# The last gate of a hybrid decoder layer as seven block products

## The chip, the core and the metric

The kernel runs on one core of a Trainium2 chip. TensorE (PE) multiplies out of the on-chip memory SBUF into the banks of PSUM; VectorE (DVE) and ScalarE (ACT) read PSUM and work elementwise in SBUF; GpSimd (POOL) does small work and issues DMAs; SyncE (SP) issues DMAs. Each engine takes its instructions in the order in which they were recorded and waits for the others by semaphores. The metric is the device time of one execution in microseconds (us). Three runs of the kernel before took 959.69, 959.97 and 960.47 us; their median is 959.97.

## What is computed

One layer on 512 tokens of 1024 features in float32: a gated linear attention beside a dilated window attention, an MLP with squared ReLU, and a gated embedding. The part that the change touches is the end:

```python
x = x + jnp.square(jax.nn.relu(h2 @ w_mlp1[i])) @ w_mlp2[i]
h3 = rmsnorm(x, ln3[i])
x = x + jax.nn.sigmoid(h3 @ w_pg[i]) * (p[i] @ w_pp[i])
return rmsnorm(x, ln_f)
```

`w_pg` is 1024 x 1024 and `w_pp` 256 x 1024. The norm of `h3` is applied late: `x * ln3` goes through the product, and the factor of each token goes into the scale of the sigmoid.

## The kernel before

**Three products for one.** Each float32 operand is split into a high part (`hi`, rounded by an ACT copy) and a low part (`lo`, a DVE subtraction), and a product is the sum of hi·hi, lo·hi and hi·lo. A weight unit is 128 x 1024: SP loads it into one of 6 raw buffers, ACT writes `hi` (L280), DVE writes `lo` (L275). `fetch` records these for one unit after the other as the products come to them, two to three units ahead.

**Seven products for eight.** Where both operands split into 2 x 2 blocks, the kernel takes Strassen's form with seven block products (`strassen`; `wide` where the weight is the moving operand and a tile has 128 tokens by 512 features). The price is sums of blocks: of weights (a DMA that adds on landing, issued by POOL at L242 and L257, or a DVE addition at L254 and L260), and of the input (`T1` to `T4`, each with splits of its own). The seven products of `wide` share the six PSUM banks of the groups a, c (pool `mm`, 4 banks, tiles `mmt`) and b (pool `sm`, tiles `smt`). A result that is finished by a later product is first copied to SBUF (`begin`) and completed by an addition from PSUM (`add`, L421).

**The order of the work.** `run` records matmuls in pieces and calls `step()` after each. A step takes one item of `later` (small work on a result) and, when enough columns have gone by, one stage of the generators in `side` (up to a `yield`). So a piece of work on ACT or DVE has a fixed place in its engine's queue, and what stands behind it waits.

**The end of the kernel before.** The second MLP product's sums go into `xx` (`finals`, L1458 and L1459). `normed` then splits each of the 8 tiles of `x * ln3` in `later`: ACT writes `hi` with the scale (L430) and a square (L461), DVE `lo` (L438) and the sum of squares (L1271). Beside the embedding product `pp` (8 tiles of 128 tokens by 512 features, 6 matmuls each, evacuated by ACT at L1531), `to_tokens` transposes `x` to tokens on PE (L1547) and ACT copies it (L1550). A `pp` tile takes one of the 4 `mm` banks; the first four take the banks that `finals` reads, the last four those of the first four. The gate `pg` is two groups of 512 features (`tmaj`), each of 4 token tiles of 24 matmuls; every tile is finished by itself: sigmoid (L1563), product with `pp` and sum (L1569, L1570), square with a row sum (L1574), and for the second group the final factor (L1590, POOL's power at L1591) and two scaled outputs (L1593 on ACT, L1599 on DVE). The last tile is cut into 384 and 128 features.

Of the kernel before, what the change touches and what calls it, by code (L numbers as in the profile page):

```python
# [19 lines left out]
P = 128  # L20
# [26 lines left out]
def weight_units():  # L47
# [7 lines left out]
    def tm(name, src, col):  # L55
        for i in range(4):
            u.append((f"{name}.{i}", "tm", src, i * 2 * P, col))

# [39 lines left out]
    for j in range(2):  # L98
        tm(f"pg{j}", "w_pg", j * 512)
# [74 lines left out]

LAST = 384
# [5 lines left out]
def block_kernel(ctx, tc, xT, ws, pT, wts, wha, wa2, vec, lnf, rel, onehot, ident_d, mask_d, out):  # L181
# [201 lines left out]
    def wide(name, xo, finish):  # L383
# [13 lines left out]
        for i, (op, xname, b) in enumerate(WIDE):  # L397
# [3 lines left out]
            for pr in range(4):  # L401
                wh, wl = weight(f"{name}.{op}.{pr // 2}")
                xh, xl = xo(xname, pr)
                r = slice((pr % 2) * 512, (pr % 2 + 1) * 512)
                mms = []
                for n in range(2):
                    c = slice(n * P, (n + 1) * P)
                    for k, (l, w) in enumerate(((xh, wh), (xl, wh), (xh, wl))):
                        mms.append((bank[b][n], l[:, c], w[:, r], fresh and not pr and not k, pr == 3 and k == 2))
                run(mms, 3, shared=True)  # L410
# [849 lines left out]

    def normed(j, col, res, acc):
# [291 lines left out]

    side.append(to_tokens())
    for g in range(2):
        tmaj(f"pp{g}", pt, evac_pp)
    ss2 = const.tile([P, 12], F32, name="ss2")
    sp2 = const.tile([P, 4], F32, name="sp2")
    fr = const.tile([P, 4], F32, name="fr")

    def gate(ps, n, tt):
        sg = u32()
        S.activation(sg[:, 0:n], ps[:, 0:n], AF.Sigmoid, scale=rt3[0][:, tt:tt + 1])  # L1563
        return sg

    def gated(sg, i, c):

        n = c.stop - c.start
        V.tensor_tensor(sg[:, 0:n], sg[:, 0:n], pps[i][:, c], op=OP.mult)  # L1569
        V.tensor_tensor(x2t[i][:, c], x2t[i][:, c], sg[:, 0:n], op=OP.add)  # L1570

    def squares(sg, i, c, col):
        n = c.stop - c.start
        S.activation(sg[:, 0:n], x2t[i][:, c], AF.Square, scale=1.0 / 32.0, accum_out=ss2[:, col:col + 1])  # L1574

    def gated_all(ps, i, tt, col):
        sg = gate(ps, 512, tt)
        gated(sg, i, slice(0, 512))
        squares(sg, i, slice(0, 512), col)

    def evac_pg0(tt, ps):
        if len(x2t) < 8:
            drain()
        gated_all(ps, tt, tt, tt)
        V.tensor_scalar(sp2[:, tt:tt + 1], ss2[:, tt:tt + 1], EPS, None, op0=OP.add)
        V.tensor_tensor(x2t[tt], x2t[tt], lnb[0], op=OP.mult)

    def scale_out(tt, col):

        V.tensor_scalar(sp2[:, tt:tt + 1], ss2[:, col:col + 1], sp2[:, tt:tt + 1], None, op0=OP.add)  # L1590
        GP.tensor_tensor(fr[:, tt:tt + 1], sp2[:, tt:tt + 1], mh[:, 0:1], op=OP.pow)  # L1591
        o = u32()
        S.activation(o, x2t[tt], AF.Copy, scale=fr[:, tt:tt + 1])  # L1593
        (S if tt == 3 else SY).dma_start(out[tt * P:(tt + 1) * P, 0:512], o)

    def put(tt, c):
        n = c.stop - c.start
        o = u32()
# [115 lines left out]
```

## Time and profile before

| | |
|---|---|
| median of three runs | 959.97 us |
| the profiled execution: its own time | 960.32 us |
| its span, first to last instruction | 958.5 us |
| PE busy (share) | 950.3 us (99%) |
| DVE busy | 739.4 us (77%) |
| ACT busy | 542.0 us (57%) |
| POOL busy | 95.3 us (10%) |
| DMA, mean | 148 GB/s |
| granted TensorE clock, mean | 0.998 |

The span is what the trace covers; the execution's own time is 1.82 us longer. A busy time is that of records whose ends are partly modelled, so a busy PE says that a matmul was under way, not how many; the distance between starts gives the rate. Waits are listed by who waited and who released.

### The profile page before, as it was taken

What the parts mean: (1) busy time and instruction counts of PE and PEld (TensorE: products, weight loads), DVE (VectorE), ACT (ScalarE), POOL (GpSimd) and SP (SyncE); (2) the same over time, 40 slices, a digit from 0 to 9 for tenths busy, and PEclk for the clock granted to TensorE, in tenths of its full rate; (3) what the DMA queues carried; (4) which work ended last, traced back from release to release, by engine and by line L of the source; (5) the groups of instructions that cost most, each with busy time, mean ns of one, the idle gap of its engine ahead of it and who ended that gap; (6) DMA issues with size and microseconds to landing.
All of it is one profiled execution on the core that took longest, in us unless ns stands there. A gap on an engine that the chain in (4) does not pass through costs nothing.

```text
span 958.5 us, 15733 instructions
## 1 busy us (share of the span) xinstructions
PE 950.3 (99%) x6230; PEld 869.3 (91%) x6230; DVE 739.4 (77%) x1060; ACT 542.0 (57%) x884; POOL 95.3 (10%) x135
## 2 busy tenths in 40 slices
PE   9999999999999999999999999999999999999997
PEld 8789998899988888999988899999998998988886
DVE  7698879866788689969755798777677899787754
ACT  7357547545674679675723456556566673354733
POOL 0140010130000012031010000101000100000000
PEclk9999999999999999999999999999999999999999
DMA  9484472973727647465645436565653473453102
GB/s 320 125 233 114 127 177 67 308 242 92 174 70 248 157 133 183 112 141 190 165 107 194 129 70 195 133 163 157 171 152 107 122 186 98 137 192 104 44 1 89
DMA packets 43723, 142.00 MB, mean 148 GB/s; under 512 B 6468, under 2 KB 7056, under 8 KB 43649
## 3 DMA queue, kind: packets, MB, share of 16 engines
q1 hardware_dynamic: 28512, 96.42, 30.1%
q0 software_dynamic: 11456, 40.07, 21.2%
q10 hardware_dynamic: 3680, 4.51, 1.3%
q8 instruction: 49, 0.80, 0.3%
q14 instruction: 26, 0.20, 0.1%
HBM read 134.64 MB, written 8.17 MB: 149 GB/s over the span
## 4 chain that ended last, share of the span: by engine, by line
PE 96%; DVE 1%; issue 1%; ACT 1%; DMA 1%; POOL 0%; POOLq 0%; DVEq 0%; ACTq 0%
PE mmt L294 80%; PE smt L294 7%; PE mmt L551 2%; PE smt L985 1%; PE smt L925 1%; PE smt L848 1%; DMA u<-y_dram 1%; PE smt L523 0%; PE smt L818 0%; PE smt L942 0%; PE smt L941 0%; PE smt L931 0%; PE smt L817 0%; PE smt L1547 0%; PE smt L1041 0%
## 5 line engine op out<-in xcount | busy, mean ns | idle before, releaser
L294 PE MATMUL mmt<-ur,hi 128*128 128x256 f32 (+1 forms) x2896 | 594.8, 303 | 0.0
L294 PEld LDWEIGHTS mmt<-ur,hi 128*128 128x128 f32 x2896 | 465.9, 188 | 21.8
L294 PE MATMUL mmt<-ur,lo 128*128 128x256 f32 (+1 forms) x1448 | 438.9, 303 | 0.0
L275 DVE TENSOR_TENSOR lo<-w,hi 128x1024 fp32r<-128x1024 f32 x250 | 303.5, 1219 | 52.3 <-PE mmt L294 30.2
L280 ACT ACTIVATE hi<-w 128x1024 fp32r<-128x1024 f32 x250 | 261.1, 1054 | 105.3 <-PE mmt L294 30.0
L294 PEld LDWEIGHTS mmt<-ur,lo 128*128 128x128 f32 x1448 | 272.7, 188 | 10.9
L294 PE MATMUL mmt<-hi,ur 128*128 128x512 f32 (+3 forms) x576 | 162.5, 367 | 0.0
L428 ACT ACTIVATE ur<-u 128x512 fp32r<-128x512 f32 x122 | 72.3, 624 | 96.8 <-DVE u L1248 30.9
L294 PEld LDWEIGHTS mmt<-hi,ur 128*128 128x128 f32 x576 | 102.5, 188 | 15.9
L294 PE MATMUL mmt<-lo,ur 128*128 128x512 f32 (+3 forms) x288 | 105.0, 365 | 0.0
L421 DVE TENSOR_TENSOR u<-u,mmt 128x512 f32<-128x512 f32 (+1 forms) x112 | 70.2, 655 | 37.1 <-PE mmt L294 36.9
L436 DVE TENSOR_TENSOR ur<-u,ur 128x512 fp32r<-128x512 f32 x121 | 79.5, 685 | 16.6 <-ACT ur L428 16.2
L368 ACT ACTIVATE u<-mmt 128x512 f32<-128x512 f32 x80 | 47.4, 593 | 47.6 <-PE mmt L294 47.3
L242 POOL DMA_DIRECT2D w<-in_wts_dram x34 | 31.3, 959 | 335.1 <-DMA w<-in_wts_dram 139.0
L294 PEld LDWEIGHTS mmt<-lo,ur 128*128 128x128 f32 x288 | 54.2, 188 | 8.6
L257 POOL DMA_DIRECT2D w<-in_wts_dram x22 | 19.6, 889 | 319.2 <-DVE w L254 231.1
L294 PE MATMUL smt<-ur,hi 128*128 128x512 f32 x160 | 50.4, 393 | 0.1
L294 PEld LDWEIGHTS smt<-ur,hi 128*128 128x128 f32 x160 | 29.7, 188 | 8.1 <-PE smt L648 0.8
L294 PE MATMUL smt<-ur,lo 128*128 128x512 f32 x80 | 31.2, 390 | 0.0
L254 DVE TENSOR_TENSOR w<-w 128x1024 f32<-128x1024 f32 x22 | 27.0, 1225 | 0.8
L260 DVE TENSOR_TENSOR w<-w 128x1024 f32<-128x1024 f32 x22 | 27.0, 1225 | 0.8
L461 ACT ACTIVATE u<-u 128x512 f32<-128x512 f32 x24 | 14.9, 621 | 16.7 <-DVE u L1329 16.7
(214 smaller groups left out, 793.2 us busy)
## 6 DMA issues: line engine op xcount, KB each, us to landing
w<-in_wts_dram SPq DMA_DIRECT2D x172, 512.0 KB, 4.4
w<-in_wts_dram POOLq DMA_DIRECT2D x56, 512.0 KB, 5.7
u<-in_xT_dram SPq DMA_DIRECT2D x8, 256.0 KB, 5.3
u<-in_ws_dram SPq DMA_DIRECT2D x8, 256.0 KB, 5.4
v_dram<-u ACTq DMA_DIRECT2D x8, 256.0 KB, 8.9
u<-v_dram POOLq DMA_DIRECT2D x8, 256.0 KB, 7.0
y_dram<-u ACTq DMA_DIRECT2D x8, 256.0 KB, 3.9
u<-y_dram POOLq DMA_DIRECT2D x8, 256.0 KB, 6.0
```

The costliest lines, as they stand in the source:

```text
L242: GP.dma_start(w, wts[UNIT[b]], accum_op=OP.add)
L254: V.tensor_tensor(w, w, raw[f"{q}.A11"], op=OP.add)
L257: GP.dma_start(w, wts[UNIT[f"{q}.A21"]], accum_op=OP.add)
L260: V.tensor_tensor(w, w, raw[f"{q}.A12"], op=OP.add)
L275: V.tensor_tensor(lo, w, hi.bitcast(F32), op=OP.subtract)
L280: S.activation(hi, w, AF.Copy)
L294: TE.matmul(o, lhsT=l, rhs=r, start=a, stop=b, skip_group_check=shared)
L368: S.activation(sums[c], bank[b], AF.Copy, scale=-scale if c[0] else scale)
L421: V.tensor_tensor(out, s, ps, op=OP.subtract if m else OP.add)
L428: S.activation(hi, x, AF.Copy)
L436: V.tensor_tensor(lo, x, hi.bitcast(F32), op=OP.subtract)
L551: TE.matmul(q0ps[i], lhsT=(hi, hi, lo)[j][:, c], rhs=(xh, xl, xh)[j], start=not k and not j, stop=k == KC - 1 and j == 2)
```

## The change

The gate becomes one `wide` group over all 1024 features: seven products of 24 matmuls of 512 columns. Its weights are 8 units of another layout, of which two are also loaded a second time and four are added to on landing, and its input sums are made by a new generator `x2sums` in `side`. `normed` keeps the scaled tile `xc` in float32 for that, and splits only the first half of the tokens where the other half is not needed. Each result's finish becomes a chain in `later`. The last product goes token tile by token tile. `gla_out`, far earlier, gets one more `yield` between its multiplications and its transposes.

```diff
-    for j in range(2):
-        tm(f"pg{j}", "w_pg", j * 512)
+    quadw("pg", "w_pg", (0, 512))
...
-    def wide(name, xo, finish):
+    def wide(name, xo, finish, by_tile=False):
...
+            last = by_tile and i == len(WIDE) - 1
+            for ns in ((0,), (1,)) if last else ((0, 1),):
+                for pr in range(4):
...
+                if last:
+                    later.append(end(*WEND[i][0], ns[0], b))
...
             if p % 2:
                 yield
+        yield
         for f in range(2):
...
+        h = slice(0, T if j % 2 else HT)
+
         def first():
-            hi, sq = split_hi(x, c), square(x)
+            xc[j] = u32()
+            S.activation(xc[j], x, AF.Copy, scale=c)
+            sq, hi, lo = square(x), u32r(), u32r()
+            S.activation(hi[:, h], xc[j][:, h], AF.Copy)
 
             def second():
-                res[j] = split_lo(x, hi, c)
+                V.tensor_tensor(lo[:, h], xc[j][:, h], hi[:, h].bitcast(F32), op=OP.subtract)
+                res[j] = hi, lo
...
+    def x2sums():
...
+        def splits(name, ts):
+            yield
+            his = [split_hi(t) for t in ts]
+            yield
+            for g in range(2):
+                t2x[name, g] = split_lo(ts[g], his[g])
+            yield
+
+        sums(lambda g, o, b11, b12, b21, b22: V.tensor_tensor(t1[g][:, o], b11, b12, op=OP.subtract))
+        yield from splits("T1", t1)
...
+    side.append(x2sums())
     side.append(to_tokens())
...
-    def evac_pg1(tt, ps):
-        gated_all(ps, 4 + tt, tt, 4 + tt)
-        scale_out(tt, 4 + tt)
-        put(tt, slice(0, 512))
-
-    tmaj("pg0", x2s, evac_pg0)
-    tmaj("pg1", x2s, evac_pg1, tts=range(3))
...
+    def gate(m, t, n, s, ps):
+
+        tt = 2 * t + n
+        i = 4 * m + tt
+        if s is None:
+            sg, z, r = u32(), ps, rtn
+            V.tensor_scalar(rtn[:, tt:tt + 1], rt3[0][:, tt:tt + 1], -1.0 if m else 1.0, None, op0=OP.mult)
+        else:
+            add(m, s, s, ps)
+            sg, z, r = s, s, rt3[0]
+
+        def gated():
+            V.tensor_tensor(sg, sg, pps[i], op=OP.mult)
+            V.tensor_tensor(x2t[i], x2t[i], sg, op=OP.add)
+            later.append(squares)
...
+        S.activation(sg, z, AF.Sigmoid, scale=r[:, tt:tt + 1])
+        later.append(gated)
+
+    wide("pg", x2_op, gate, by_tile=True)
+    flush()
```

Where this puts instructions is seen in three places. Line numbers are those of each program. The first is ACT's queue between the last tile of `normed` and the split of the gate's first weights; before (L430 `hi`, L461 squares, L1550 token copies, L1531 evacuations of `pp`, L280 weights):

```order
L430 ACTIVATE ur<-u,cv 128x512
L461 ACTIVATE u<-u 128x512
L1550 ACTIVATE u<-smt 128x512
L1531 ACTIVATE u<-mmt 128x512
L1550 ACTIVATE u<-smt 128x512
L1531 ACTIVATE u<-mmt 128x512
L1550 ACTIVATE u<-smt 128x512
L1531 ACTIVATE u<-mmt 128x512
L1550 ACTIVATE u<-smt 128x512
L280 ACTIVATE hi<-w 128x1024 x2
```

and now (L1272 the scaled copy `xc`, L1274 its `hi`, L1540 evacuations, L1559 token copies, L428 the `hi` of T1, L273 weights):

```order
L1272 ACTIVATE u<-u,cv 128x512
L461 ACTIVATE u<-u 128x512
L1274 ACTIVATE ur<-u 128x512
L1540 ACTIVATE u<-mmt 128x512
L1559 ACTIVATE u<-smt 128x512
L1540 ACTIVATE u<-mmt 128x512
L428 ACTIVATE ur<-u 128x512 x2
L1540 ACTIVATE u<-mmt 128x512
L1559 ACTIVATE u<-smt 128x512
L273 ACTIVATE hi<-w 128x1024 x2
L1540 ACTIVATE u<-mmt 128x512 x2
```

A tile has three ACT passes where it had two, and the third and fourth evacuations stand behind the `hi` of T1 and two weight splits. The second place is DVE's queue from the last addition of squares to the gate's first weights; before (L438 `lo`, L1271 squares, L275 weights, L455 the norm's factor):

```order
L438 SCALAR_TENSOR_TENSOR ur<-u,cv,ur 128x512
L1271 TENSOR_TENSOR u<-u 128x512
L275 TENSOR_TENSOR lo<-w,hi 128x1024 x2
L455 TENSOR_SCALAR rv<-smt 128x4
L275 TENSOR_TENSOR lo<-w,hi 128x1024 x2
```

and now (L1584 and L579 the sums T1 and T2, L436 the `lo` of a sum, L244 a weight sum):

```order
L1277 TENSOR_TENSOR ur<-u,ur 128x512
L1280 TENSOR_TENSOR u<-u 128x512
L1584 TENSOR_TENSOR u<-u 128x256 x4
L268 TENSOR_TENSOR lo<-w,hi 128x1024 x2
L436 TENSOR_TENSOR ur<-u,ur 128x512 x2
L579 SCALAR_TENSOR_TENSOR u<-u 128x256 x4
L268 TENSOR_TENSOR lo<-w,hi 128x1024
L244 TENSOR_TENSOR w<-w 128x1024
L436 TENSOR_TENSOR ur<-u,ur 128x512 x2
L268 TENSOR_TENSOR lo<-w,hi 128x1024
```

The sums and their splits stand between the weights' `lo`. The third place is DVE's end; before (L1569, L1570 the gate, L1590 and L1622 the final factor, L1599 an output):

```order
L1599 SCALAR_TENSOR_TENSOR u<-u,fr 128x512
L1569 TENSOR_TENSOR u<-u 128x384
L1570 TENSOR_TENSOR u<-u 128x384
L1569 TENSOR_TENSOR u<-u 128x128
L1570 TENSOR_TENSOR u<-u 128x128
L1622 TENSOR_SCALAR sp_9784<-ss_9783,sp_9784 128x1
L1590 TENSOR_SCALAR sp_9784<-ss_9783,sp_9784 128x1
L1599 SCALAR_TENSOR_TENSOR u<-u,fr 128x256 x2
```

and now, from the sixth product's results on (L1627 the output weights of the first 512 features, L1614 the negated token factor that the last sigmoids read, L1620 and L1621 the gate, L1633 the final factor, L1645 an output):

```order
L1627 TENSOR_TENSOR u<-u 128x512 x2
L1614 TENSOR_SCALAR rtn<-rtok 128x1
L1633 TENSOR_SCALAR sp_9800<-ss_9799,sp_9800 128x1 x2
L1620 TENSOR_TENSOR u<-u 128x512
L1621 TENSOR_TENSOR u<-u 128x512
L1645 SCALAR_TENSOR_TENSOR u<-u,fr 128x512
L1614 TENSOR_SCALAR rtn<-rtok 128x1
L1645 SCALAR_TENSOR_TENSOR u<-u,fr 128x512
L1620 TENSOR_TENSOR u<-u 128x512
L1621 TENSOR_TENSOR u<-u 128x512
L1633 TENSOR_SCALAR sp_9800<-ss_9799,sp_9800 128x1
L1645 SCALAR_TENSOR_TENSOR u<-u,fr 128x512
```

The factor of the last token tile's sigmoid stands behind the output of another tile, and its own chain is followed by one more sum, a power and two halves of an output.

## Rows read from the trace of the kernel before

**Rows 1.** The page: busy time, share and instructions of each engine.

```profile
PE 950.3 (99%) x6230; PEld 869.3 (91%) x6230; DVE 739.4 (77%) x1060; ACT 542.0 (57%) x884; POOL 95.3 (10%) x135
```

**Rows 2.** PE's waits: us in total, times, the longest.

```profile
PE smt L523 <- POOL ones L518: 1.0, 1, 1.0
PE smt L1140 <- DVE u L1133: 0.2, 1, 0.2
```

**Rows 3.** Stretches: length; busy of PE, PEld, DVE, ACT, POOL; PE clock; DMA.

```profile
432.00:470.00 38.00, 37.84 (x318) 37.26 (x317) 35.75 (x49) 24.63 (x41) 2.43 (x4) 1.00 0.62 188
...
891.00:905.70 14.70, 14.70 (x82) 12.52 (x81) 12.33 (x18) 13.50 (x24) 1.95 (x1) 1.00 0.19 68
905.70:944.40 38.70, 38.70 (x177) 32.07 (x176) 18.95 (x29) 15.94 (x28) 1.10 (x2) 1.00 0.04 16
```

**Rows 4.** The chain that ended last, from 890: start, us, what.

```profile
901.18 0.79 PE smt L468 x8
...
907.57 0.87 PE smt L1547 x8
908.44 36.33 PE mmt L294 x160
```

**Rows 5.** ACT in order of time: start, us, line, operation, count.

```profile
881.14 0.71 ACT L430 ACTIVATE ur<-u,cv 128x512 fp32r<-128x512 f32 x1
881.75 0.62 ACT L461 ACTIVATE u<-u 128x512 f32<-128x512 f32 x1
882.27 0.71 ACT L430 ACTIVATE ur<-u,cv 128x512 fp32r<-128x512 f32 x1
...
891.01 0.73 ACT L430 ACTIVATE ur<-u,cv 128x512 fp32r<-128x512 f32 x1 [7.51 <-DVE u L1459]
...
899.42 2.05 ACT L280 ACTIVATE hi<-w 128x1024 fp32r<-128x1024 f32 x2
```

**Rows 6.** DVE in order of time.

```profile
884.42 2.49 DVE L1432 TENSOR_TENSOR u<-u,rstd 128x512 f32<-128x512 f32 x4
886.83 2.77 DVE L1441 TENSOR_TENSOR u<-u 128x256 f32<-128x256 f32 x8
889.51 0.68 DVE L1458 TENSOR_TENSOR u<-mmt,rstd 128x512 f32<-128x512 f32 x1
...
894.82 0.75 DVE L438 SCALAR_TENSOR_TENSOR ur<-u,cv,ur 128x512 fp32r<-128x512 f32 x1
...
899.88 2.36 DVE L275 TENSOR_TENSOR lo<-w,hi 128x1024 fp32r<-128x1024 f32 x2
```

**Rows 7.** PE in order of time: `pp`'s first tile; the cut tile's two ends.

```profile
891.03 0.39 PE L294 MATMUL mmt<-hi,ur 128*128 128x512 f32 x1
...
944.37 0.56 PE L294 MATMUL mmt<-hi,ur 128*128 128x512 f32 x2
...
951.30 0.28 PE L294 MATMUL mmt<-hi,ur 128*128 128x128 f32 x1
```

**Rows 8.** A group by shape over the whole program: busy, mean ns; idle before.

```profile
L1072 ACT ACTIVATE ur<-u 128x256 fp32r<-128x256 f32 x12 | 4.2, 414 | 0.4 <-DVE u L1070 0.4
```

**Rows 9.** The end of a tile and of the program in order of time.

```profile
944.79 0.69 ACT L1563 ACTIVATE u<-mmt,rtok 128x512 f32<-128x512 f32 x1 [0.90 <-PE mmt L294]
945.52 0.69 DVE L1569 TENSOR_TENSOR u<-u 128x512 f32<-128x512 f32 x1 [1.59 <-ACT u L1563]
946.25 0.69 DVE L1570 TENSOR_TENSOR u<-u 128x512 f32<-128x512 f32 x1
946.97 0.63 ACT L1574 ACTIVATE u<-u 128x512 f32<-128x512 f32 x1 [1.48 <-DVE u L1570]
...
947.73 0.21 DVE L1590 TENSOR_SCALAR sp<-ss,sp 128x1 f32<-128x1 f32 x1 [0.79 <-ACT u L1574]
948.02 0.54 POOL L1591 TENSOR_TENSOR fr<-sp,mh 128x1 f32<-128x1 f32 x1 [4.88 <-DVE sp L1590]
...
953.97 0.88 DVE L1599 SCALAR_TENSOR_TENSOR u<-u,fr 128x256 f32<-128x256 f32 x2 [0.66 <-POOL fr L1591]
```

More of the change, by code (lines that the diff above doesn't have):

```diff
@@ L53, in fm @@
             u.append((f"{name}.{j}", "fm", src, row, col + j * P))
-    def tm(name, src, col):
-        for i in range(4):
-            u.append((f"{name}.{i}", "tm", src, i * 2 * P, col))
     def quad(name, src, col, kind="quad", chunk=0):
@@ L173 @@
 NRAW = 6
-LAST = 384
 NWARM = 9
@@ L400, in wide @@
                 bank[b] = [smt() if b == "b" else mmt() for _ in range(2)]
[L401 to L410, printed above, removed]
+            last = by_tile and i == len(WIDE) - 1
+            for ns in ((0,), (1,)) if last else ((0, 1),):
+                for pr in range(4):
+                    wh, wl = weight(f"{name}.{op}.{pr // 2}")
+                    xh, xl = xo(xname, pr)
+                    r = slice((pr % 2) * 512, (pr % 2 + 1) * 512)
+                    mms = []
+                    for n in ns:
+                        c = slice(n * P, (n + 1) * P)
+                        for k, (l, w) in enumerate(((xh, wh), (xl, wh), (xh, wl))):
+                            mms.append((bank[b][n], l[:, c], w[:, r], fresh and not pr and not k, pr == 3 and k == 2))
+                    run(mms, 3, shared=True)
+                if last:
+                    later.append(end(*WEND[i][0], ns[0], b))
+            if last:
+                break
             if i in WBEGIN:
@@ L1556, in block_kernel @@
         tmaj(f"pp{g}", pt, evac_pp)
-    ss2 = const.tile([P, 12], F32, name="ss2")
+    ss2 = const.tile([P, 8], F32, name="ss2")
     sp2 = const.tile([P, 4], F32, name="sp2")
     fr = const.tile([P, 4], F32, name="fr")
[L1561 to L1598, printed above, removed]
-        V.scalar_tensor_tensor(out=o[:, 0:n], in0=x2t[4 + tt][:, c], scalar=fr[:, tt:tt + 1], in1=lnb[1][:, c],
-                               op0=OP.mult, op1=OP.mult)
-        SY.dma_start(out[tt * P:(tt + 1) * P, 512 + c.start:512 + c.stop], o[:, 0:n])
@@ L1620, in block_kernel, with squares, total, put @@
-    squares(sgs[0], 7, parts[0], 8)
-    gated(sgs[1], 7, parts[1])
-    V.tensor_scalar(sp2[:, 3:4], ss2[:, 8:9], sp2[:, 3:4], None, op0=OP.add)
-    squares(sgs[1], 7, parts[1], 9)
-    scale_out(3, 9)
-    put(3, slice(256, 512))
-    put(3, slice(0, 256))
+    rtn = const.tile([P, 4], F32, name="rtn")
+    halves_done = [0] * 4
+    def gate(m, t, n, s, ps):
[11 more added lines that the diff above has]
+            later.append(squares)
+        def squares():
+            S.activation(sg, x2t[i], AF.Square, scale=1.0 / 32.0, accum_out=ss2[:, i:i + 1])
+            if not m:
+                V.tensor_tensor(x2t[i], x2t[i], lnb[0], op=OP.mult)
+            later.append(total)
+        def total():
+            first = not halves_done[tt]
+            halves_done[tt] += 1
+            V.tensor_scalar(sp2[:, tt:tt + 1], ss2[:, i:i + 1], EPS if first else sp2[:, tt:tt + 1], None, op0=OP.add)
+            if not first:
+                GP.tensor_tensor(fr[:, tt:tt + 1], sp2[:, tt:tt + 1], mh[:, 0:1], op=OP.pow)
+                later.append(put)
+        def put():
+            tok, c = slice(tt * P, (tt + 1) * P), fr[:, tt:tt + 1]
+            o = u32()
+            S.activation(o, x2t[tt], AF.Copy, scale=c)
+            (S if tt == 1 else SY).dma_start(out[tok, 0:512], o)
+            for h in ((slice(256, 512), slice(0, 256)) if tt == 1 else (slice(0, 512),)):
+                q = u32()
+                V.scalar_tensor_tensor(out=q[:, h], in0=x2t[4 + tt][:, h], scalar=c, in1=lnb[1][:, h], op0=OP.mult,
+                                       op1=OP.mult)
+                SY.dma_start(out[tok, 512 + h.start:512 + h.stop], q[:, h])
+        S.activation(sg, z, AF.Sigmoid, scale=r[:, tt:tt + 1])
+        later.append(gated)
```

28 lines of the change are left out of this document (19 added, 9 removed).

## The prediction

> **What bounds the kernel now.** I read the page first, then PE's waits, then stretches of the end, and then ACT, DVE and PE in order of time. The page gives PE 950.3 of 958.5 us, all others at most 77% [rows 1]. PE's waits show two entries for the whole program, 1.0 us at the start and 0.2 us at the transpositions of L1140 [rows 2]. So PE is never short of operands, and what is left is its 1 us at the start and the 7 us after its last matmul. The chain says the same: from 908.44 on, 160 matmuls follow each other in 36.33 us, 0.227 us each [rows 4]. A change that takes matmuls away therefore gains, as long as the other engines still finish in PE's shadow. How much shadow there is in the last 70 us I take from the stretches: ACT is busy for 13.50 of the 14.70 us in which `pp` runs (891.0 to 905.7), DVE for 12.33; in the gate itself DVE for 18.95 and ACT for 15.94 of 38.70 [rows 3]. The room is in the gate, not in `pp`.
>
> **What goes on PE.** The gate has 8 tiles of 24 matmuls before, 7 products of 24 now. The missing tile is in effect the one cut in two: its first matmul of 384 columns starts 0.23 us after 944.37 and its last ends at 951.58, so 7.0 us go [rows 7]. The transpositions stay (0.87 us a group with the change of work around it, 0.79 us for the norm's sums [rows 4]); two of the four groups and the sums now fall among the gate's products.
>
> **What comes, by instruction.** ACT: a third pass for each of the 8 tiles of `normed`, 8 `hi` of sums, 6 more weight `hi`. DVE: 16 half-width sums of the input, 8 `lo` of sums, 6 more weight `lo`, 4 weight sums, 6 additions from PSUM. As distance from start to start: DVE 0.60 us for 512 columns ((2.49-0.68)/3), 0.34 for 256 ((2.77-0.42)/7), 1.14 for a weight `lo` (2.36-1.22) [rows 6]; 0.73 where one waits for its own predecessor (945.52 to 946.25) [rows 9]. ACT 0.61 for a pass with a scale, 0.52 for one without, about 0.31 for half a tile (0.41 less the same overlap) [rows 5, 8]; 0.98 for a weight `hi` (2.05-1.07) [rows 5]. I take a weight sum as a weight `lo`. Six more weight transfers cost nothing: the DMA share is 0.04 in the gate [rows 3]; without that cover a product would wait for 512 KB, 3.5 us at the mean of 148 GB/s.
>
> **Step 1, the first half of `normed`.** The tiles split at 881 need 1.65 us of ACT each, not 1.13. The second one's `hi` ends at 881.14+1.65+1.13+0.62 = 884.5, and DVE's `lo` and sum behind it end the pair at 885.8, where the block of L1432 stood at 884.42 [rows 5, 6]. So `finals` begin 1.4 us late, at 890.9. The first of them frees the bank of `pp`'s first tile at 891.6; PE wants it at 891.03 [rows 7]. PE waits 0.6.
>
> **Step 2, `pp`.** ACT's tiles start at 891.01+1.35 = 892.35 and take 2x1.65+2x1.44 = 6.2, to 898.5; the first evacuation ends at 899.1. PE's fifth tile needs that bank, and is due at 891.6+4x1.36+0.87 = 897.9: a wait of 1.2. DVE ends `finals` at 890.9+5.3 = 896.2 (889.51 to 894.82 before [rows 6]), the four `lo` and square sums at 900.5, the four sums T1 at 901.85. ACT's two `hi` of T1 stand before the third evacuation, which so ends at 903.05; PE's seventh tile is due at 902.7: a wait of 0.35. Before the fourth evacuation stand a token copy and two weight `hi` (0.48+1.96): it ends at 905.9, the eighth tile is due at 904.4: a wait of 1.5. The waits sum to 3.7 us, and the gate begins at 907.3. No row of before shows a wait on a bank of PSUM, so the bounds are 0 and 3.7; I take 3.7, since all of it is queue order times measured durations.
>
> **Step 3, the products.** 168x0.227 = 38.15, plus two groups of transpositions and the norm's sums, 2.5: PE ends at 948.0, 3.6 us earlier than now.
>
> **Step 4, DVE behind the products.** From 890.9 to the end of the fourth product DVE has 37.2 us of work (`finals` 5.3, `lo` and squares 4.3, 16 sums 5.6, 8 `lo` 4.8, 11 weight `lo` 12.5, 4 weight sums 4.7) in 40 us, so it arrives just in time. The fourth product's first result is ready at 907.3+4x5.45+2.5-0.6 = 931.0. From there DVE has: the fourth product's two additions to 932.4, its two gates (0.73+0.60 each) to 935.1, a weight `lo` 936.3, two output weights 937.5, a weight `lo` 938.8. The fifth product ended at 937 and waits: additions to 940.0, 0.25 for the sigmoid, gates to 942.9, the last weight `lo` to 944.1. The sixth ended at 942.5: additions to 945.5, gates to 948.35, output weights with a wait for the second square to 949.8, then the token factor. Only now (950.0) may the sigmoid of the seventh product's first tile start, although PE finished that tile at 945: sigmoid 0.7, gate to 952.0, an earlier tile's output 952.7, the second token factor 952.85. Its sigmoid ends at 953.55, the gate at 954.95, the square (0.63 and its read, to DVE's start 0.76 later [rows 9]) at 955.7. DVE has put the first tile's output before the second's final sum: 956.3, sum 956.55, power 0.55, two half outputs 0.88: 958.0. Before, that last instruction ends at 953.97+0.88 = 954.85 [rows 9]. So the end is 3.1 us later, though PE is 3.6 us earlier.
>
> **The sum.** +3.1, +0.2 since two token tiles (1 MB) leave in the last 2 us where it was one, -0.2 for the transpositions of L1140, if the extra `yield` takes all of that wait [rows 2]; bounds of the last two: 0 to 0.7 and -0.2 to 0. That is 3.1 us on the profiled execution's 960.32, or 0.3%, and on the median of 959.97: **963.1 us**. Durations not shown before: the sigmoid out of SBUF (0.62 as a plain pass, 0.69 as L1563), the small token factors (0.15 to 0.21), together at most 0.6 us on the last chain. `pT` is now issued behind a weight addition on POOL; I cost this at nothing because ACT, its first reader, still idles 7.51 us before `pp` [rows 5], and at some 1 us if it came later than that.
>
> **Rivals.**
> *DVE's queue swallows the waits (no measurable change).* If `pp`'s evacuations come in time, PE gains 3.7, but DVE has only 40-37.2 = 2.8 us of air before the fourth product, so the end moves by 2 to 3 us at most: about 960.5. For it: before, ACT evacuates in a row without PE ever waiting. Against it: the queue order above, in which evacuations stand behind T1.
>
> *PE sets the end (faster).* In another stretch, 432 to 470, a `wide` group runs with DVE busy 35.75 of 38.00 us and PE waits only 0.16 [rows 3]: the form itself can be fed. If DVE keeps up here too, PE begins the gate at 903.6, ends at 944.3, and after it come one sigmoid, gate, square, sum, power and output at full width, 0.73+1.46+0.76+0.29+0.57+0.88 = 4.7 [rows 9]: the last output ends at 949.0, 5.9 earlier, so 954.1. It decides from the point where DVE's work per product stays under a product's 5.45 us. By step 4 it is 7.8 us in the fourth and 5.5 and 5.7 in the next two, so what DVE falls behind it does not make up.
>
> *The clock falls in `pp` (much slower).* The granted clock is 1.00 in all these stretches, the level of 2.4 GHz [rows 3]. Four waits between 891 and 906 would be the first close together. If the level of 1.2 GHz were granted for one product's length, 5.45 us of products would take 10.9: 968.6. The Trainium skill, TensorE: Matmul & The Clock Gate, section A second HAM failure mode: psum-queue depth-cycling, tells of just that, PE idling briefly again and again over PSUM banks until the clock goes up and down. By that rule the time is this rival's; the trace of before has no such waits and can't show it.
>
> **How the numbers follow.** Within about 0.2% (1.9 us) a measurement of this kernel can't tell from no change. The forecast, ACT's and DVE's queues end later, 0.60, its own range 961.3 to 965.0. No measurable change 0.22, around 960.5. PE sets the end or most of it 0.13, 953 to 958. The clock 0.05. The forecast's lower edge lies within 0.2%, so a tenth of it counts as no change. Faster 0.13, same 0.28, slower 0.59. The range takes the forecast, the second rival whole and leaves out the far ends: 958.0 to 965.8.
>
> **What would show it.** Right: PE waits on ACT's evacuations of `pp` (some 3 us, two or three of them over 1 us) and one short wait on DVE's `finals`; the gate's products start near 907 and PE's last matmul ends near 948; DVE is busy almost without a gap from 931; the last sigmoids start only after the small token factor on DVE, and DVE's last output ends some 10 us after PE's last matmul, where it was 3.3. Wrong: PE's waits stay under 0.5 us, or the sixth product's additions start as soon as it ends; then PE's gain of 7 us comes through. If the granted clock is below 1 around 900 to 910, the third rival holds.

## The result, and the profile after

The changed kernel takes 962.94 us (median of 8 runs, 962.47 to 963.36), the kernel before 959.76 us in runs beside it (8 runs, 959.52 to 960.63). The ratio is 1.0029, 95% interval 1.002 to 1.0039: slower by 3.2 us. The forecast was 963.1.

| profiled execution | before | after |
|---|---|---|
| span | 958.5 us | 961.2 us |
| PE busy | 950.3 us | 943.6 us |
| last matmul ends | 951.6 | 947.4 |
| last output of DVE ends | 954.85 | 957.61 |

The page of the changed kernel, which answers to [rows 1]:

```profile
PE 943.6 (98%) x6182; PEld 861.3 (90%) x6182; DVE 762.8 (79%) x1099; ACT 557.6 (58%) x909; POOL 98.1 (10%) x139
```

PE lost 48 matmuls and 6.7 us of work, DVE gained 23.4 us and ACT 15.6. PE's waits in the changed kernel (us in total, times, longest), which answer to [rows 2]:

```profile
PE mmt L287 <- ACT u L1540: 2.1, 2, 1.2
PE smt L523 <- POOL ones L518: 1.0, 1, 1.0
PE mmt L287 <- DVE u L1467: 0.4, 1, 0.4
PE smt L925 <- DVE u L905: 0.2, 1, 0.2
```

The wait at the transpositions is gone. Two on ACT's evacuations of `pp` (L1540) and one on DVE's `finals` (L1467) are new (the 0.2 us at L925 lie before 270 us, far from the change). Here are the three, and the tile that begins without a listed wait, in PE's order of time (start, us, line, operation, idle before it):

```profile
890.38 0.50 PE L287 MATMUL mmt<-hi,ur 128*128 128x512 f32 x1 [0.38 <-DVE u L1467]
...
897.92 0.50 PE L287 MATMUL mmt<-hi,ur 128*128 128x512 f32 x1 [0.87 <-ACT u L1540]
...
901.86 0.50 PE L287 MATMUL mmt<-hi,ur 128*128 128x512 f32 x1
...
904.73 0.50 PE L287 MATMUL mmt<-hi,ur 128*128 128x512 f32 x1 [1.21 <-ACT u L1540]
```

The starts tell more than the brackets. From the first to the fifth tile lie 7.54 us; four tiles of 1.36 and one group of transpositions of 0.87 are 6.31, so 1.23 us were lost, not 0.87. From the fifth to the seventh it is 3.94 against 3.59, from the seventh to the eighth 2.87 against 1.36. These three sum to 3.1 us where the view lists 2.1. The difference has two parts. The last matmul before the fifth tile starts at 896.67 and the next would be due 0.23 us later, so PE stood still for 1.02 us up to 897.92; the view begins to count only at that matmul's modelled end, 0.39 us after its start, and lists 0.87. In the same way the other two stops are 0.28 us (not listed) and 1.38 (listed as 1.21), and the one before the first tile is 0.54 (listed as 0.38). The rest is lost without a stop, most of it because the first matmul behind each is followed after 0.34 us and not 0.23.

Why the evacuations came late stands in ACT's rows of the same stretch:

```profile
897.30 0.57 ACT L1540 ACTIVATE u<-mmt 128x512 f32<-128x512 f32 x1
...
900.02 1.30 ACT L428 ACTIVATE ur<-u 128x512 fp32r<-128x512 f32 x2 [1.19 <-DVE u L1584]
901.23 0.58 ACT L1540 ACTIVATE u<-mmt 128x512 f32<-128x512 f32 x1
...
902.19 2.00 ACT L273 ACTIVATE hi<-w 128x1024 fp32r<-128x1024 f32 x2
904.08 1.08 ACT L1540 ACTIVATE u<-mmt 128x512 f32<-128x512 f32 x2
```

The first evacuation begins only at 897.30, behind the eight tiles of `normed`. The third stands behind the `hi` of T1 (L428), which itself waits 1.19 us for DVE's block sums (L1584), the fourth behind two weight `hi`. Stretches of the changed kernel (length; PE, PEld, DVE, ACT, POOL; clock; DMA), which answer to the last two of [rows 3]:

```profile
891.00:907.00 16.00, 13.89 (x67) 10.75 (x66) 14.41 (x28) 14.69 (x28) 0.00 (x0) 1.00 0.01 1
907.00:931.00 24.00, 24.00 (x120) 20.13 (x119) 22.36 (x31) 17.57 (x27) 2.02 (x2) 1.00 0.41 110
931.00:948.00 17.00, 16.42 (x72) 13.04 (x70) 16.23 (x27) 9.75 (x19) 0.00 (x0) 1.00 0.00 0
```

In the gate DVE is now busy 38.59 of 41 us, where it was 18.95 of 38.70. What that makes of the end, in DVE's and ACT's order of time (answers to [rows 9]):

```profile
943.47 1.28 DVE L421 TENSOR_TENSOR u<-u,mmt 128x512 f32<-128x512 f32 x2
...
949.09 0.15 DVE L1614 TENSOR_SCALAR rtn<-rtok 128x1 f32<-128x1 f32 x1
949.33 0.69 ACT L1649 ACTIVATE u<-mmt,rtn 128x512 f32<-128x512 f32 x1 [0.88 <-DVE rtn L1614]
...
952.05 0.14 DVE L1614 TENSOR_SCALAR rtn<-rtok 128x1 f32<-128x1 f32 x1
952.28 0.69 ACT L1649 ACTIVATE u<-mmt,rtn 128x512 f32<-128x512 f32 x1 [1.51 <-DVE rtn L1614]
...
956.73 0.88 DVE L1645 SCALAR_TENSOR_TENSOR u<-u,fr 128x256 f32<-128x256 f32 x2 [0.66 <-POOL fr L1635]
```

PE's last matmul ends at 947.4, but the last tile's sigmoid starts at 952.28, on a factor of one column that DVE reaches only behind the sixth product's gates and an output. From PE's end to DVE's last output it is 10.2 us; before it was 3.3.

### The profile page after: what moved, and what is told of

It is laid out like the page before. It is cut to its first block, busy times and chain, and to the rows that moved or that the text cites. A ratio compares the mean times of both kernels' runs of the same rounds, so it can differ in the third digit from the quotient of the medians.

```text
span 961.2 us, 15716 instructions
## 1 busy us (share of the span) xinstructions
PE 943.6 (98%) x6182; PEld 861.3 (90%) x6182; DVE 762.8 (79%) x1099; ACT 557.6 (58%) x909; POOL 98.1 (10%) x139
## 4 chain that ended last, share of the span: by engine, by line
PE 92%; DVE 5%; ACT 2%; issue 1%; POOL 0%; POOLq 0%; DVEq 0%; ACTq 0%
PE mmt L287 76%; PE smt L287 6%; PE mmt L551 2%; PE smt L985 1%; PE smt L925 1%; PE smt L848 1%; DVE lo L268 1%; DVE u L1620 1%; DVE ur L436 1%; DVE u L1621 0%; PE smt L523 0%; DVE u L421 0%; ACT hi L273 0%; ACT ur L428 0%; ACT u L1649 0%
## 5 line engine op out<-in xcount | busy, mean ns | idle before, releaser
L268 DVE TENSOR_TENSOR lo<-w,hi 128x1024 fp32r<-128x1024 f32 x256 | 311.4, 1221 | 48.7 <-PE mmt L287 29.6
L273 ACT ACTIVATE hi<-w 128x1024 fp32r<-128x1024 f32 x256 | 267.9, 1055 | 104.1 <-PE mmt L287 29.9
L287 PE MATMUL mmt<-hi,ur 128*128 128x512 f32 (+1 forms) x528 | 151.2, 371 | 2.5 <-ACT u L1540 2.1
L428 ACT ACTIVATE ur<-u 128x512 fp32r<-128x512 f32 x130 | 77.3, 626 | 98.8 <-DVE u L1249 30.9
L287 PEld LDWEIGHTS mmt<-hi,ur 128*128 128x128 f32 x528 | 93.9, 188 | 19.2 <-ACT u L1540 3.2
L421 DVE TENSOR_TENSOR u<-u,mmt 128x512 f32<-128x512 f32 (+1 forms) x116 | 72.9, 657 | 36.4 <-PE mmt L287 36.0
L436 DVE TENSOR_TENSOR ur<-u,ur 128x512 fp32r<-128x512 f32 x129 | 84.9, 689 | 17.7 <-ACT ur L428 17.2
L287 PE MATMUL mmt<-lo,ur 128*128 128x512 f32 (+1 forms) x264 | 97.2, 368 | 0.0
L235 POOL DMA_DIRECT2D w<-in_wts_dram x38 | 34.8, 952 | 383.4 <-DMA w<-in_wts_dram 174.6
L287 PEld LDWEIGHTS mmt<-lo,ur 128*128 128x128 f32 x264 | 49.6, 188 | 8.4 <-DVE lo L268 0.3
L250 POOL DMA_DIRECT2D w<-in_wts_dram x22 | 19.6, 891 | 316.4 <-DVE w L247 230.3
L461 ACT ACTIVATE u<-u 128x512 f32<-128x512 f32 x24 | 14.9, 620 | 16.7 <-DVE u L1338 16.7
```

What stands on the lines that cost most here:

```text
L235: GP.dma_start(w, wts[UNIT[b]], accum_op=OP.add)
L250: GP.dma_start(w, wts[UNIT[f"{q}.A21"]], accum_op=OP.add)
L268: V.tensor_tensor(lo, w, hi.bitcast(F32), op=OP.subtract)
L273: S.activation(hi, w, AF.Copy)
L287: TE.matmul(o, lhsT=l, rhs=r, start=a, stop=b, skip_group_check=shared)
L421: V.tensor_tensor(out, s, ps, op=OP.subtract if m else OP.add)
```

## The experiments

My theory throughout: the end follows the queues of ACT (in `pp`) and DVE (from there on), not PE's work. All but the changed kernel itself were timed in five rounds beside the kernel before; the column on the right is against the kernel before of the same batch, so that kernels of different batches can be compared.

| kernel | us | ratio, 95% | us against before |
|---|---|---|---|
| changed kernel | 962.94 | 1.0029 (1.002 to 1.0039) | +3.18 |
| before with the extra `yield` | 959.23 | 0.999 (0.9982 to 0.9999) | -0.71 |
| no block sums | 960.66 | 1.0007 (0.9998 to 1.0016) | +0.72 |
| block sums later | 960.86 | 1.001 (1.0001 to 1.0019) | +0.92 |
| factors at once | 962.21 | 1.002 (1.0011 to 1.0028) | +2.27 |
| output weights on POOL | 963.49 | 1.004 (1.0026 to 1.0053) | +3.52 |
| scaled copies on POOL | 962.86 | 1.0038 (1.0026 to 1.0049) | +2.89 |
| four edits | 961.04 | 1.0014 (1.0005 to 1.0023) | +1.07 |
| five edits | 961.82 | 1.002 (1.0011 to 1.0029) | +1.85 |
| token squares | 957.67 | 0.9977 (0.9968 to 0.9987) | -2.31 |
| all outputs together | 958.11 | 0.998 (0.9971 to 0.9989) | -1.87 |
| outputs in pairs | 957.64 | 0.9973 (0.9964 to 0.9983) | -2.34 |
| before with token squares | 959.93 | 1.0001 (0.9992 to 1.001) | +0.08 |

**The extra yield alone.** The kernel before with one line more, ahead of the transpositions:

```
                 yield
+        yield
         for f in range(2):
```

> The kernel before with one part of the change alone: the extra yield ahead of the transpositions of L1140; gate, pp and normed as before. By the waits view of before (0.2 us on DVE in that place) the gain is at most 0.2 us: 959.6. By the view of that line, which says that PE idles there 4 times for 0.9 us in the mean, more than the waits view lists because modelled ends of matmuls cover it, the stretch 430 to 440 holds about 5 more matmuls and the program ends 0.6 to 0.9 us earlier: 958.9 to 959.2. If the yield moves nothing that PE waits for, 959.8.

Measured 959.23, 0.71 us less than before. The stretch 430 to 440, first of the kernel before, then of this one:

```profile
430.00:440.00 10.00, 9.84 (x82) 9.41 (x81) 8.05 (x12) 4.31 (x9) 3.53 (x7) 1.00 0.97 312
```

```profile
430.00:440.00 10.00, 10.00 (x87) 10.00 (x86) 7.92 (x11) 4.59 (x9) 3.37 (x7) 1.00 0.93 308
```

Five more matmuls fit, though PE's busy time grew by 0.16 us only. The view of that line in the kernel before has the sum right:

```profile
its engine sat idle before it (us, times) until:
  DVE u L1133: 0.9, 4
```

It is 0.9 us over all four times (the expectation calls it a mean, wrongly; its numbers go by the total). The waits view lists one of the four, with 0.2 us.

**The block sums taken out, and begun later.** In the first the products with T1 to T4 take B11:

```
-        return cols(t2x[name, pr // 2], halves(pr % 2))
+        if name[0] == "T":
+            name = "B11"
...
-    side.append(x2sums())
```

> The changed kernel without the block sums of the gate's input and their splits (16 half-width sums and 8 lo on DVE, 8 hi on ACT go); the products with T1 to T4 take the block B11 instead, so the gate's values are not the reference's; PE's instructions are the same. My theory (the queues of ACT and DVE set the end): in pp the waits on the third and fourth evacuation of ACT go, the one on DVE's finals and the first on ACT stay, so the gate begins about 1.5 to 2 us earlier, and the program ends about 2 us earlier: 960.7 (960.2 to 961.5). It does not fall under 960, since the queue of DVE behind the fourth product stays as it is. Rival, the end depends on the sums through all of DVE's 10.4 us of work before the fourth product: 957 or less. Rival, the sums hide beside PE altogether: 962.9.

In the second the sums stay, but begin two steps later:

```
     def x2sums():
+        for _ in range(2):
+            yield
```

> The changed kernel with the block sums begun two side steps later (two empty yields ahead of them), so that in ACT's queue the evacuations of pp stand ahead of the hi of T1. My theory: PE's third and fourth wait on ACT's evacuations in pp go (1.2 us and some 0.3 us), the gate begins 1.5 us earlier, and since DVE has 2.8 us of air before the fourth product, the end follows by 1.5 to 1.8 us: 961.2. Rival, DVE has no air and the later sums are late for the gate's T products: 962.9 or more, with a new wait of PE on DVE's split of T1 or T2 in the gate.

Measured 960.66 and 960.86: 2.5 and 2.3 us less than the changed kernel. PE's waits without the sums, then with the sums later:

```profile
PE mmt L287 <- ACT u L1540: 0.4, 1, 0.4
PE mmt L287 <- DVE u L1467: 0.4, 1, 0.4
```

```profile
PE mmt L287 <- ACT u L1540: 0.8, 1, 0.8
PE mmt L287 <- DVE u L1467: 0.4, 1, 0.4
```

In both the waits on the third and fourth evacuation are gone (the one that is left stands ahead of the fifth tile, at 898.35 and 897.59), and the stretch from PE's last matmul to DVE's last output stays at 10.2 us (945.14 to 955.31 and 945.23 to 955.44). So the sums cost what they push aside in ACT's queue: taking 10.4 us of DVE's work away gains no more than moving it by two steps. (Without the sums the token transpositions come a step earlier too, which is why the first wait is shorter there.) What pushes is the `hi` of T1 and its wait for DVE. In the kernel with the sums later two weight `hi` still stand ahead of the fourth evacuation, and PE does not wait for it:

```profile
899.35 2.01 ACT L273 ACTIVATE hi<-w 128x1024 fp32r<-128x1024 f32 x2
901.25 1.09 ACT L1540 ACTIVATE u<-mmt 128x512 f32<-128x512 f32 x2
```

The three rivals (no effect, an effect of all of DVE's work, a new wait on T) are out.

**The factors at once.** One instruction right behind `rt3`, in place of one ahead of each last sigmoid:

```
                 rt3.append(rms_tok(acc2[0]))
+                V.tensor_scalar(rtn[:, 0:4], rt3[0][:, 0:4], -1.0, None, op0=OP.mult)
...
-            V.tensor_scalar(rtn[:, tt:tt + 1], rt3[0][:, tt:tt + 1], -1.0 if m else 1.0, None, op0=OP.mult)
```

> The changed kernel with the four negated token factors (rtn) made in one instruction right behind rt3, not one by one in DVE's queue before each last sigmoid. My theory: the sigmoids of the seventh product's tiles no longer stand behind DVE's gates, the first starts when its bank is done, and the end comes 1.0 us earlier: 961.9 (961.3 to 962.3); PE's waits in pp stay (2.5 us). Rival, DVE's own work, not the place of the factor, sets the end: the gate on DVE starts no earlier, under 0.3 us: 962.7 to 962.9.

Measured 962.21, 0.9 us nearer to the kernel before. By the times alone the intervals overlap. The trace tells it apart: from PE's last matmul to DVE's last output it is 9.2 us (947.88 to 957.05), 1.0 less than in the changed kernel. The last two sigmoids still wait, now behind ACT's squares and an output copy.

**Work moved to POOL.** Four output weights (L1627):

```
-                V.tensor_tensor(x2t[i], x2t[i], lnb[0], op=OP.mult)
+                GP.tensor_tensor(x2t[i], x2t[i], lnb[0], op=OP.mult)
```

> The changed kernel with the four output weights (x2t times lnb[0], L1627) on POOL, not on DVE. They take DVE 4 times 0.6 us behind the fourth product, two of them after the sixth product's gates, where nothing but DVE's queue is late. My theory (that queue sets the end): 2.0 us earlier, 960.9, if POOL takes no more than 1 to 2 us for one; no row of the trace shows POOL multiplying 128x512 values, the nearest is its fill of such a tile in 0.70 us. PE's waits in pp stay. Rival, POOL is so slow that the scaled copy of the third and fourth token tile waits for it: later than 962.9. Rival, the end hangs on ACT's sigmoid alone: 962.9.

Measured 963.49: no gain, where 2 us were expected. POOL and DVE beside it, then the last weight `lo` and PE's load of it:

```profile
934.24 3.87 POOL L1627 TENSOR_TENSOR u<-u 128x512 f32<-128x512 f32 x2 [18.84 <-ACT u L1625]
```

```profile
934.64 2.32 DVE L268 TENSOR_TENSOR lo<-w,hi 128x1024 fp32r<-128x1024 f32 x1
936.89 0.20 DVE L1633 TENSOR_SCALAR sp<-ss 128x1 f32<-128x1 f32 x2
937.01 2.18 DVE L268 TENSOR_TENSOR lo<-w,hi 128x1024 fp32r<-128x1024 f32 x1
...
943.25 1.22 DVE L268 TENSOR_TENSOR lo<-w,hi 128x1024 fp32r<-128x1024 f32 x1
944.38 0.21 DVE L1633 TENSOR_SCALAR sp<-ss 128x1 f32<-128x1 f32 x2
944.52 0.19 PEld L287 LDWEIGHTS mmt<-lo,ur 128*128 128x128 f32 x1 [1.17 <-DVE lo L268]
```

A weight `lo` takes 1.22 us elsewhere in this window and 2.32 and 2.18 beside POOL's multiplications. DVE saves 0.6 us for each that it gives away and loses 1.0 to 1.1 beside each of the first two (of the last two only one meets a DVE instruction of this kind, a gate's product of 1.53 us instead of 0.69). PE waits 0.7 us more, listed under L1633, a total that DVE does next; the late one is the `lo` ahead of it, which PE's weight load names. This is what the Trainium skill, SBUF — State Buffer, section Who interferes with whom, states: an instruction of VectorE with two inputs in SBUF contends with a GpSimd instruction that reads SBUF. The trace agrees: these instructions take 0.8 to 1.1 us longer. My theory named DVE's queue rightly and had the price of POOL wrong.

Then the eight scaled copies of `normed`:

```
-            S.activation(xc[j], x, AF.Copy, scale=c)
-            sq, hi, lo = square(x), u32r(), u32r()
-            S.activation(hi[:, h], xc[j][:, h], AF.Copy)
+            GP.tensor_scalar(xc[j], x, c, None, op0=OP.mult)
+            hi, lo = u32r(), u32r()
+            S.activation(hi[:, h], x[:, h], AF.Copy, scale=c)
+            sq = square(x)
```

> The changed kernel with the eight scaled copies of the input (xc) on POOL, not on ACT; hi and lo are made from the input and the factor in one pass each as in the kernel before, but still half as wide for the even tiles. My theory: ACT's third pass for each tile is what delays finals and the first evacuation, so PE's wait on DVE's finals (0.4 us) and the one on the first evacuation (1.2 us) go; the waits on the third and fourth evacuation stay, since they come from the hi of T1 and the weights ahead of them, and take over part of the time gained. Gate and end 1.0 to 1.5 us earlier: 961.7. Rival, all of pp's waits come from the third pass: the gate 2.5 us earlier, 960.4. Rival, POOL is slow and T1 waits for it: 963 or more.

Measured 962.86: nothing gained. Its waits (the 0.3 us lie between 400 and 500 us, far from the edit):

```profile
PE mmt L287 <- ACT u L1542: 2.9, 2, 1.8
PE mmt L287 <- DVE lo L268: 0.3, 1, 0.3
```

The waits on `finals` and on the first evacuation are gone, as expected, so ACT's third pass was their cause. But from the start of `finals` to T1 DVE takes 10.7 us (889.06 to 899.77), where it takes 9.6 in the changed kernel, and the evacuations behind T1's `hi` are later than before (waits of 1.8 and 1.1 us). What was won there was lost again, and 962.86 is nearly the 963 of the third expectation. Its cause, T1 waiting for POOL, is not what the trace shows. POOL takes 1.7 us for each of the last four copies and is done with them at 897.32, while DVE comes to T1 without a gap:

```profile
890.56 6.76 POOL L1272 TENSOR_SCALAR u<-u,cv 128x512 f32<-128x512 f32 x4 [11.13 <-DVE u L1470]
...
893.98 0.91 DVE L1470 TENSOR_TENSOR u<-u 128x512 f32<-128x512 f32 x1
...
895.80 1.18 DVE L1278 SCALAR_TENSOR_TENSOR ur<-u,cv,ur 128x512 fp32r<-128x512 f32 x1
...
899.77 1.42 DVE L1586 TENSOR_TENSOR u<-u 128x256 f32<-128x256 f32 x4
```

DVE is late itself: beside POOL's copies two of its `finals` take 0.91 us instead of 0.69 and one `lo` 1.18 instead of 0.74, and a `lo` made from input and factor in one pass takes some 0.06 longer. So this is the contention of the run before again, smaller.

The profiled execution of this kernel shows one thing more. It took 966.17 us, the other five 962.40 to 963.30. Behind the first of the two waits the granted clock fell to the lower level, 1.2 GHz:

```profile
902.45 0.50 PE L287 MATMUL mmt<-hi,ur 128*128 128x512 f32 x1 [1.77 <-ACT u L1542]
...
905.32 0.80 PE L287 MATMUL mmt<-hi,ur 128*128 128x512 f32 x1 [1.11 <-ACT u L1542]
905.91 0.63 PE L287 MATMUL mmt<-lo,ur 128*128 128x512 f32 x1
906.34 1.05 PE L287 MATMUL mmt<-hi,ur 128*128 128x512 f32 x2
```

```profile
904.00:910.00 6.00, 4.89 (x12) 3.72 (x12) 5.97 (x10) 6.00 (x11) 0.00 (x0) 0.50 0.00 0
```

The granted clock is 0.50 from 903.9 to 910.7, and matmuls start 0.43 us apart there, not 0.23. From 905.32 on that costs PE 2.7 us, most of what this execution is longer.

**Four and five edits.** The four are the two on POOL, the factors and the later sums; the fifth is

```
-                    later.append(end(*WEND[i][0], ns[0], b))
+                    later.insert(0, end(*WEND[i][0], ns[0], b))
```

> Four edits at once in the changed kernel: output weights and scaled copies on POOL, the factors made early, the block sums two side steps later. If all that separates it from the kernel before stands in the queues of ACT and DVE, PE has no wait left in pp, the gate begins at 903.5 (changed kernel 906.0) and the end comes 5 to 6 us earlier than in the changed kernel: 957.1 (956.3 to 958.5), under the kernel before. If one limit lies behind the others (PE's end and the chain of one tile after it: 944.6 and 4.7 us) it can't be under 954.

> As the kernel with four edits, and the last product's first tile is put ahead of what is left in the list of later steps, so that its sigmoid stands in ACT's queue ahead of the squares of the sixth product's tiles. My theory: 1.0 to 1.3 us earlier than with four edits, 955.9 (955.3 to 957.0). Rival, the sigmoid ahead of the squares waits for PE and holds them up, and DVE with them: no gain or some 0.5 us lost, 957.1 to 957.6.

Measured 961.04 and 961.82, 4 and 6 us over what was expected. In `pp` the theory held: PE has no wait there. In the gate POOL's multiplications made DVE late for a weight `lo` (listed under the total behind it, as above), the same row in both:

```profile
PE mmt L287 <- DVE sp L1637: 2.0, 1, 2.0
```

With five edits the gate of the last product's first tile fell beside POOL on DVE (1.76 and 1.63 us for what takes 0.69), and the outputs then left all at once: the DMAs were busy at 1.00 to 1.04 from 952 to 957. That was a limit I had not thought of.

**DVE's work cut, nothing on POOL.** The norm's sum of squares comes from the token copies, which ACT can sum while it squares them; the token copies go ahead of the block sums, and the factors are made at once as above:

```
+        for i in range(8):
+            q = u32()
+            S.activation(q, x2t[i], AF.Square, scale=1.0 / 32.0, accum_out=ss3[:, i:i + 1])
+            yield
...
-                if j:
-                    V.tensor_tensor(acc[0], acc[0], sq, op=OP.add)
...
-    side.append(x2sums())
     side.append(to_tokens())
+    side.append(x2sums())
```

> The changed kernel with DVE's work cut where the runs so far put the bound: the sum of squares for the gate's norm comes from the token copies (8 squares of ACT with an accumulated sum, in place of 8 squares, 7 additions of 0.6 us on DVE and the norm's sums on PE), the token copies go ahead of the input's block sums, and the negated factors are made at once. Nothing is put on POOL. My theory (DVE's queue is the bound from pp on, and PE waits in pp come from ACT's third pass, square and hi of T1 ahead of the evacuations): no wait of PE in pp, the gate begins near 903, one wait of about 1 us on the last weight's lo in the gate, DVE's last output 4.2 us earlier than in the changed kernel, 958.8 (958.0 to 959.8). Rival, ACT, which gets 8 squares with a read of their sums more in the gate, takes DVE's place as the bound: 960.5 or more.

Measured 957.67, 2.3 us under the kernel before and 5.5 under the changed one: 1.1 earlier than expected and just under the range given (958.0 to 959.8). PE has no wait in `pp` and 0.2 us in the gate:

```profile
PE mmt L287 <- DVE sp L1637: 0.2, 1, 0.2
```

Its last matmul ends at 943.3, DVE's last output at 952.4. The rival, ACT as the new bound, is out by its time (960.5 or more). ACT is nearly full from 907 to 931, 21.98 of 24 us, but PE does not wait there; from 931 to 945 it is busy for 7.26 of 14 us, DVE for 13.28.

**The order of the outputs.** On top of it, all gates first, or three gates, two outputs, the last gate:

```
+        if last:
+            tail.append((gated, squares, total, output_weight, put))
...
+    for k, ns in ((0, range(4)), (1, range(4)), (2, (0, 1)), (3, (0, 1)), (2, (2, 3)), (4, range(4))):
+        for n in ns:
+            tail[n][k]()
```

> As the kernel with token squares, and DVE's order behind the sixth product written out: all four gates, then totals, output weights and the four outputs one behind the other, so that no gate stands behind an output. By DVE's queue alone its last output comes 1.7 us earlier: 957.0. Rival, the output DMAs: in the kernel with five edits they were busy at 1.00 from 952 to 957 with 2 MB, and here too all 2 MB leave behind the last gate, from some 1.4 us behind the first output's start on, 5.6 us of transfer and 1.6 us to the end: 959.4, no gain against the kernel with token squares.

> As the kernel with token squares, and DVE's order behind the sixth product: three gates, then the outputs of the third and fourth token tile, then the last gate and the outputs of the first two. Both theories at once: 1 MB leaves while DVE still works on the last gate, so the output DMAs don't bind, and DVE's last output comes 0.8 us earlier than with token squares: 957.9 (957.2 to 958.8). If the end went with DVE's queue alone, this kernel would be later than the one with all outputs together; if it goes with the DMAs, earlier by some 1.5 us.

Measured 958.11 and 957.64. With all outputs together DVE ends 2.1 us earlier than with token squares (950.34 against 952.42), and the span is the same, 956.0 against 956.1. The last stretches, first with token squares, then with all outputs together:

```profile
949.00:954.00 5.00, 0.00 (x0) 0.00 (x0) 2.11 (x6) 2.17 (x4) 1.08 (x2) 0.50 0.84 308
```

```profile
949.00:954.00 5.00, 0.00 (x0) 0.00 (x0) 1.34 (x3) 1.05 (x2) 0.29 (x1) 0.50 1.03 377
```

At 377 GB/s 2 MB take 5.6 us. With all outputs together the DMAs are full for the whole stretch and the program ends some 5.7 us behind DVE (950.34 to 956.0), with token squares 3.7. So the rival holds in its cause: the output DMAs took the place of DVE's queue. Its 959.4 was 1.3 us too late. In pairs the end is 0.5 us earlier than together, where 1.5 were expected if the DMAs decide, and the two intervals overlap; it is no earlier than with token squares (957.64 against 957.67). DVE's last output comes 0.2 us earlier in pairs, not the 0.8 expected, and that is within the scatter.

**The same in the kernel before.** Its gate left as it was:

> The kernel before with the extra yield and with the squares from the token copies, its gate left as it was (eight tiles of 24 matmuls). It tells whether the gain of the kernel with token squares needs the gate of seven products. My theory (in the kernel before PE is the bound and DVE has room, so 4 us less on DVE gain nothing; the norm's sums on PE, 0.79 us, go, but all squares now lie in ACT's queue in pp, where ACT is full, and the first gate tile's sigmoid waits for the factors): between nothing and 1.2 us later than the kernel before with the yield alone, 959.2 to 960.4. Rival, the gain belongs to the token squares and not to the gate: 958.0 or less.

```
-            hi, sq = split_hi(x, c), square(x)
+            hi = split_hi(x, c)
...
+                    S.activation(q, t, AF.Square, scale=1.0 / 32.0, accum_out=ss3[:, i:i + 1])
```

Measured 959.93, as the kernel before, and 0.7 over the one with the extra `yield` alone. PE waits 0.8 us for a weight's `lo`, since ACT is busy for 4.00 of the 4 us from 903 to 907 and its `hi` come late. So the gain of the kernel with token squares needs the gate of seven products, in which DVE is the bound. The wait is a cost of this order of the squares; without its 0.8 us the kernel would be at 959.1 by an estimate, no better than with the extra `yield` alone.

## Why the prediction was right

- **What goes on PE.** 7.0 us said, 6.7 by the page.
- **Step 1.** `finals` begin at 889.64. The trace of after runs 1.24 us ahead of that of before by then (`normed`'s last pair starts at 879.90, was 881.14), and with that the step's 890.9 is 889.66. Taking ACT's third pass away removed the wait.
- **Step 2.** 3.7 us said; by the starts of the four tiles 0.6 for the first (890.38 against 891.03-1.24) and 3.1 for the others, of which 3.2 in all are stops of PE. The waits view lists 2.5. Of the causes named, T1's `hi` is shown by the two kernels in which it is gone or stands elsewhere. The two weight `hi` alone are none: with the sums later they still stand ahead of the fourth evacuation, and PE does not wait.
- **Step 3.** PE ends 0.6 us later than said, with the 1.24 us taken off: 947.4 against 946.8. By the starts, 0.16 of it is there when the gate begins (906.22 against 906.06); the two groups of transpositions and the norm's sums take 0.2 more than the 2.5 said, the last matmul counts with 0.39 us and not 0.23, and 0.15 is lost at 943.49, where PE meets the last weight's `lo`.
- **Step 4.** The places are as said: additions to the sixth product begin at 943.47 (said 944.1), the first token factor ends at 949.24 (950.0), the second at 952.19 (952.85), the last output at 957.61 (958.0). With the 1.24 taken off the forecast, each comes 0.5 to 0.85 us later than said. Of that 0.5 is there already at the fourth product, where DVE waits for PE (its additions begin at 930.27, said 931.0). Making the factors at once took 1.0 us from the end.
- **The small terms.** The extra `yield` was mis-sized: 0.2 us was taken from the waits view, alone it measures 0.7. The waits view had hidden three of the four stops there, so the reading that PE is never short of operands was wrong by that much. The added 0.2 for two token tiles' output did not come: from DVE's last output to the end it is 3.6 us in both. Without the yield's 0.7 the measured 3.2 us would be 3.9, against 3.3 by the terms said (3.1 and 0.2), if the two add up. The yield's extra 0.5 and the later end nearly cancel, so that the sum came within 0.2 us of the measured time is in part luck. Some 0.6 us of the 1.24 lie in the first 27 us of the program, where a group of 96 matmuls (L551) took 22.8 us before and 22.1 after with nothing changed; the kernels with token squares and with the two output orders differ there by as much (21.90 to 22.50). The cause is the clock's first rise: in the trace of before the group's matmuls still start 0.43 us apart until 6.5 us, the pace of the level of 1.2 GHz, and in that of after 0.23 apart from 5.4 on.

**The rivals.** *DVE's queue swallows the waits* asked that the evacuations come in time, and said 960.5. With the sums two steps later they nearly do, and the time is 960.86: its price was about right, its condition did not hold. (It is the first in the prediction's list; the remark on the range, which calls the rival that it takes whole the second, means this one.) *PE sets the end* is out, since PE ends 10.2 us ahead of DVE. *The clock falls in `pp`*: in the changed kernel the granted clock is 1.00, the level of 2.4 GHz, from 891 to 948, although PE stopped for a PSUM bank four times in 15 us, for 0.28 to 1.38 us; in all of its eight runs the mean granted clock is 0.994 or 0.995. By the Trainium skill (TensorE: Matmul & The Clock Gate, section A second HAM failure mode: psum-queue depth-cycling) such stops make the clock go up and down; here they did not. But the rival is not out for kernels like this one. In the profiled execution with scaled copies on POOL, PE stood still in `pp` for 2.0 and 1.4 us, and the clock fell for 6.8 us, which cost PE 2.7. The length of a stop alone does not decide: with four edits PE stood still for 2.2 us at 939, and the clock stayed at 1.00 up to PE's end. What decides no run here shows.

What the change could have brought is shown by the kernel with token squares: the seven products gain 2.3 us against the kernel before, and 1.6 against it with the extra `yield`, once DVE has less to do. A lower limit from PE's end alone (943.3 and the 4.7 us of one tile's chain) was not reached; the outputs' 5.6 us of transfer and DVE's queue stand in between.

## What to carry to other kernels

A form with fewer matmuls moves its cost to the engines that make and take its sums: count their work per product against the product's length, and follow the queue to the last output, since an instruction of one column can stand behind microseconds of others. Measure a wait by the distance between starts of the waiting engine, and use the list of waits only to find who is waited for. Before work is moved to an idle engine, ask what it shares with the busy one, and before outputs are bunched, what their transfer takes.

## What the runs showed of the hardware

- The waits view misses 0.15 to 0.17 us of each wait of PE by the starts of matmuls: stops of 0.54, 1.02 and 1.38 us were listed as 0.38, 0.87 and 1.21, one of 0.28 was not listed. The first matmul behind a stop is followed after 0.34 us, not 0.23.
- In one execution (scaled copies on POOL) the granted clock fell from 1.00 to 0.50 for 6.8 us, from 903.9 on, after PE had stood still for 2.0 us up to 902.45. In the changed kernel, with stops of up to 1.38 us, and with four edits, with one of 2.2, it stayed at 1.00.
- POOL takes 1.4 to 1.9 us for a 128x512 multiplication of two fp32 tensors and 1.6 to 1.7 with a factor per partition, against 0.6 on DVE. Beside the first kind a DVE instruction with two SBUF inputs took 0.8 to 1.1 us longer (0.69 to 1.53 and 1.76, 1.22 to 2.32), beside the second some took 0.2 to 0.4 longer (0.69 to 0.91, 0.74 to 1.18).
- The DMAs of the output run at 377 GB/s with a busy share of 1.03, so the last 2 MB of a program cost 5.6 us when they leave together.
